# A list-scheduled hybrid decoder step: the scheduler's idea of pauses and landings is changed, half-partition work goes from VectorE to ScalarE and TensorE, and the last scale is kept in PSUM

## The chip, the cores and the metric

One core of a Trainium2 chip runs the whole step in one launch. The metric is the device time of that launch in microseconds (us), over several runs. PE is TensorE, DVE is VectorE, ACT is ScalarE, POOL is GpSimd, SP is the engine that issues most DMAs; PEld is TensorE's weight load.

## The reference

One layer of a decoder for 256 prompt tokens and 8 x 8 sample tokens (320 columns in all), width 2048, all in fp32:

```python
proj = rms_norm(x, ln1_g) @ w_in                     # 2048 -> 7440 columns
o_a = gdn_mixer(...)                                  # 8 gated-DeltaNet heads, chunks of 64 tokens
o_b = rwkv_mixer(...)                                 # 16 RWKV-7 heads, one state of 64 x 64 each
x = x + concatenate([o_a, o_b]) @ w_o
f = (silu(gate) * up) @ w_down                        # gate, up = causal_dwconv(rms_norm(x) @ w_up)
y = rms_norm(x + f, final_g)
```

Both mixers return their recurrent states too. The delta rule needs the solution of a triangular system for each chunk, the RWKV-7 part a state per head, which this kernel updates chunk by chunk: s = decay * (s + k^T u).

## The kernel before

Activations lie transposed, 128 features on partitions and 320 tokens in a row. Each weight piece of 128 x 512 is loaded by SP (`raw`), copied by ACT to a rounded `whi` (line 539) and subtracted by DVE to the rest `wlo` (line 548); PE multiplies `whi` with the high and low part of the activation and `wlo` with the high part (`stream`, lines 554 to 583), so every 128 x 128 tile of weights costs three matmuls of 320 columns. There are 3648 such matmuls up to the end of `w_o` and 6336 in the FFN behind it.

The work before the FFN is the projection, in an order that mixes RWKV pairs of heads (R0 to R7), GDN pairs (G0 to G3) and gates (Z0 to Z3), with the mixers' own small work running between the projection's matmuls. `rwkv` (line 1077) and `gdn` (line 1568) do one pair each: element work on DVE and ACT, a 32 x 32 block solve on DVE (`solve`, line 1374: tiles `xt`, 62 short instructions) with a way through DRAM in front and behind (`scr`, `scx`, `gscr`, `gscx`), a step that joins the blocks on PE (lines 1255 to 1264 and 1678 to 1694), and then four chunks, each of which needs the state that the one before it left (lines 1272 to 1305 and 1702 to 1740).

No engine's order is written by hand. `Prog` (line 167) runs the generators of all parts side by side, keeps a clock for each engine (`clk`), and a time at which every operand is ready (`ready`, line 195: the writer's planned end and a latency from `LAT`, line 104). At each step `run` (line 316) takes of every engine the instruction that can begin first, and appends it to the program. The weight stream has the lowest rank (1000), so it fills PE's planned gaps; its rank is raised when PE would otherwise do too little or has just come back to it (line 337, `vg`). The chip keeps that order on each engine and waits where the plan was too early. Numbers that steer the plan are in `CFG` (line 96). `begin` (line 220) says when an instruction can start: when its engine's clock is past the one before and its operands are ready. `dma` (line 474) plans a landing by bytes, with an additional `lag` where one is given; `dl` is what a DMA adds for its readers.

In the state step of `rwkv` (lines 1285 to 1298) PE forms k^T u in PSUM (`pb`); DVE multiplies the old state by the decay (line 1289) and then adds the decayed product, once for each half of the partitions (line 1298).

At the end, `rms_last` (line 885) gives 1/rms in `rs2`, and 16 tiles are scaled by it: nine by DVE, four by POOL, and the last three by DVE together with the gain (`last`, line 1014). Each goes out by its own DMA, from SP and ACT in turn (lines 1022 to 1024).

Of the kernel before, what the change touches and what calls it, by code (L numbers as in the profile page):

```python
# [19 lines left out]
P = 128  # L20
NTOK = 320
# [74 lines left out]
CFG = dict(es=0, eg=1, ln=1, bl=0, re=(7,), rg=1, gp={3: 5}, nw=(3, 4), b5=4, b4=4, b2=6, c2=9, b1=12, bi=8, raw=7, xt=2, ord='R0 R1 G0 R2 R3 Z0 G1 R4 R5 Z1 G2 R6 R7 Z2 G3 Z3', dl=1900, wr=2, l2=300, ra=3, war=1, vt=150, lw=1, lh=2, s1=9, st=6, m=80, ev=50, sp=0, cv=0, pq=1000, ug=1, sg=0, gv=1023, fs=105, pl=3000, pd=1000, pr=0.4605, ch=100, gs=1.0, hw=3400, ha=0.45, vg=700, pq2=0, fa=1, lk=1)  # L96
# [9 lines left out]


# [59 lines left out]
class Prog:  # L167
    def __init__(self, tc, a, ctx):
# [5 lines left out]
        self.port = {"V": 0.0, "G": 0.0}  # L174
        self.shape, self.work, self.full, self.left_at = (128, 128), [], True, -1e9
# [44 lines left out]
    def begin(self, op):  # L220

        t = max(self.clk[op.key], op.ready)
        return max(t, self.port["G" if op.key == "V" else "V"]) if op.port else t

# [7 lines left out]
    def emit(self, th):  # L232
        op = th.op
        op.fn()
        t = self.begin(op)
        if op.port:
            self.port[op.key] = t + op.cost
# [290 lines left out]
    def wload(self):  # L528
        for p, (ap, w) in enumerate(self.raws):
            t = yield from self.take(self.raw_s, 1)  # L530
            yield self.dma(t[:, :w], ap)
            self.nload = p + 1
            self.raw[p] = t
# [236 lines left out]
    def main(self):  # L770
# [43 lines left out]
        def keys(n, slots):  # L814
            for k in WO[n]:
# [5 lines left out]
                if m is None:  # L821
                    yield self.dma(lo, self.dmx[k])
# [44 lines left out]
        rs2 = fp.tile([P, NTOK], F32, name="rs2")  # L867
        yield self.ms(G, ssa, 0.0)
# [16 lines left out]
        def rms_last(t):  # L885
# [5 lines left out]
            yield from self.rstd(g[:, :NTOK], rs2)  # L891
            self.flags.add("rs2")

# [183 lines left out]
    def rwkv(self, i, box):  # L1077
# [7 lines left out]
        yield self.dma(lw, self.a["lw"][i])  # L1085
# [72 lines left out]
        for h in range(2):  # L1158
            s = slice(64 * h, 64 * h + 64)
            yield self.tt(V, ar[s, :, 0, h], c64(kk)[s], c64(e0)[s], ALU.mult)  # L1160
# [100 lines left out]
        yield self.cp(V, pt_, g[hi, 0:256])  # L1261
# [726 lines left out]
```

## Time and profile before

| what | value |
|---|---|
| three runs | 1780.39, 1783.66 and 1785.14 us, median 1783.66 |
| profiled execution, its own time | 1782.98 us |
| its span (first to last instruction) | 1781.2 us |
| busy share of the span | PE 95%, PEld 92%, DVE 72%, ACT 55%, POOL 10% |
| granted TensorE clock, mean | 0.988 |
| DMA | 256.52 MB, mean 144 GB/s |

The span falls into four stretches by time from its start: the first loads (0 to 36 us), projection and mixers with `w_o` (36 to 834), the FFN (834 to 1766), and the last norm with its stores (1766 to 1781.2). A busy PE says little here, since matmuls overlap each other in the records; what PE waits for and what the other engines do in the second stretch has to be read apart.

### The profile page before, as it was taken

How to read it: one execution, taken by the hardware profiler on the slowest of the kernel's cores; microseconds unless marked ns; L12 is line 12 of the kernel's file. 1: busy time of each engine (PE TensorE's matmuls, PEld its weight loads, DVE VectorE, ACT ScalarE, POOL GpSimd, SP SyncE). 2: the span in 40 equal slices, each digit the busy share in tenths (PEclk: the TensorE clock that was granted, in tenths of full speed). 3: DMA queues.
4: the chain of work that ended last, by engine and by line, in shares of the span. 5: the costliest groups of instructions: out<-in, count | busy, mean ns of one | idle time of the engine just before them, and what ended most of it. 6: DMA issues, size and time to landing. Idle time of an engine off the chain costs nothing.

```text
span 1781.2 us, 33357 instructions
## 1 busy us (share of the span) xinstructions
PE 1700.1 (95%) x11959; PEld 1635.1 (92%) x11959; DVE 1285.2 (72%) x3447; ACT 982.2 (55%) x2281; POOL 180.1 (10%) x482
## 2 busy tenths in 40 slices
PE   8999999899989989999999999999999999999996
PEld 7998889788978888799999999999999999999996
DVE  7989888788978799778766666644466666665444
ACT  7776847575666566546545445433345545455442
POOL 0200000000000000113111111100001111110001
PEclk9999999999999999999999999999999999999998
DMA  6434424344424446355444444455444444445554
GB/s 223 134 126 132 134 95 139 105 134 124 142 82 137 126 125 208 98 187 169 154 148 149 154 147 151 147 152 148 146 155 152 152 146 153 151 147 150 150 144 141
DMA packets 103830, 256.52 MB, mean 144 GB/s; under 512 B 32048, under 2 KB 43056, under 8 KB 103664
## 3 DMA queue, kind: packets, MB, share of 16 engines
q1 hardware_dynamic: 102512, 253.08, 45.5%
q8 instruction: 94, 1.54, 0.4%
q10 hardware_dynamic: 1152, 1.31, 0.2%
q14 instruction: 72, 0.59, 0.1%
HBM read 239.13 MB, written 15.22 MB: 143 GB/s over the span
## 4 chain that ended last, share of the span: by engine, by line
PE 69%; DVE 17%; DMA 7%; ACT 3%; issue 2%; SPq 1%; POOL 0%; DVEq 0%; ACTq 0%; POOLq 0%
PE mm L384 26%; PE rA L384 20%; PE rB L384 19%; DVE wlo L436 4%; PE g L384 3%; DVE b L436 3%; DVE xt L436 2%; DMA b<-scr 2%; ACT b L413 2%; DVE h L436 1%; DMA b<-scx 1%; DVE bi L431 1%; DMA b<-srw 1%; DVE c L431 1%; DVE b L431 1%
## 5 line engine op out<-in xcount | busy, mean ns | idle before, releaser
L413 ACT ACTIVATE whi<-raw 128x512 fp32r<-128x512 f32 (+2 forms) x842 | 520.4, 621 | 592.8 <-PE mm L384 227.8
L436 DVE TENSOR_TENSOR wlo<-raw,whi 128x512 fp32r<-128x512 f32 (+2 forms) x842 | 576.4, 686 | 323.9 <-ACT whi L413 317.3
L384 PE MATMUL mm<-h,whi 128*128 128x320 f32 x2992 | 693.3, 315 | 0.0
L384 PEld LDWEIGHTS mm<-h,whi 128*128 128x128 f32 x2992 | 509.5, 191 | 2.2 <-issue 0.5
L384 PE MATMUL mm<-h,wlo 128*128 128x320 f32 x1496 | 473.4, 316 | 5.0 <-DVE wlo L436 4.9
L384 PEld LDWEIGHTS mm<-h,wlo 128*128 128x128 f32 x1496 | 285.4, 191 | 8.7 <-DVE wlo L436 7.2
L384 PE MATMUL rB<-h,whi 128*128 128x320 f32 x1136 | 250.6, 309 | 0.0
L384 PE MATMUL rA<-h,whi 128*128 128x320 f32 x1136 | 250.6, 309 | 0.0
L384 PEld LDWEIGHTS rB<-h,whi 128*128 128x128 f32 x1136 | 189.8, 188 | 0.1
L384 PEld LDWEIGHTS rA<-h,whi 128*128 128x128 f32 x1136 | 189.8, 188 | 0.0
L384 PE MATMUL rB<-h,wlo 128*128 128x320 f32 x568 | 175.6, 309 | 0.4 <-DVE wlo L436 0.4
L384 PE MATMUL rA<-h,wlo 128*128 128x320 f32 x568 | 175.3, 309 | 0.0
L449 POOL COPY sfo<-f 128x18 f32<-128x18 f32 x88 | 61.3, 697 | 688.6 <-DVE f L436 688.6
L384 PEld LDWEIGHTS rB<-h,wlo 128*128 128x128 f32 x568 | 106.5, 188 | 0.8 <-DVE wlo L436 0.7
L384 PEld LDWEIGHTS rA<-h,wlo 128*128 128x128 f32 x568 | 106.5, 188 | 0.0
L431 DVE SCALAR_TENSOR_TENSOR f<-f,vec,f 128x336 f32<-128x336 f32 x176 | 102.6, 583 | 3.4
L436 DVE TENSOR_TENSOR b<-b,b 80x60 f32<-80x60 f32 (+28 forms) x303 | 80.2, 266 | 9.2 <-ACT b L413 3.7
L384 PE MATMUL rB<-fx,whi 128*128 128x320 f32 x336 | 74.1, 309 | 0.0
L384 PE MATMUL rA<-fx,whi 128*128 128x320 f32 x336 | 74.1, 308 | 0.0
L384 PE MATMUL rA<-b,b 128*32 128x128 f32 (+3 forms) x488 | 56.7, 289 | 15.7 <-DMA b<-srw 5.3
L384 PEld LDWEIGHTS rA<-b,b 128*32 128x32 f32 (+2 forms) x488 | 43.0, 154 | 23.2 <-issue 14.0
L436 DVE TENSOR_TENSOR xt<-xt,b 80x60 f32<-80x60 f32 (+21 forms) x248 | 48.3, 206 | 13.4 <-DMA b<-scr 12.3
(263 smaller groups left out, 2370.2 us busy)
## 6 DMA issues: line engine op xcount, KB each, us to landing
raw<-w_up SPq DMA_DIRECT2D x176, 512.0 KB, 3.7
raw<-w_in SPq DMA_DIRECT2D x116, 512.0 KB, 4.0
raw<-w_dn SPq DMA_DIRECT2D x64, 512.0 KB, 3.5
raw<-w_dn SPq DMA_DIRECT2D x32, 384.0 KB, 3.0
raw<-w_oa SPq DMA_DIRECT2D x16, 512.0 KB, 4.5
b<-sgdn SPq DMA_DIRECT2D x8, 512.0 KB, 5.2
o_sgs<-b SPq DMA_DIRECT2D x8, 512.0 KB, 4.6
raw<-w_ob SPq DMA_DIRECT2D x8, 512.0 KB, 3.8
```

Source lines behind the costliest of these rows:

```text
L384: op = Op("T", cost, (out,), (lhsT, rhs), lambda: self.nc.tensor.matmul(out, lhsT, rhs, start=start, stop=stop))
L413: lambda: self.nc.scalar.activation(out, in_, func, **kw), {AF.Exp: "E", AF.Ln: "L", AF.Silu: "S", AF.Tanh: "T"}.get(func))
L431: lambda: self.V.scalar_tensor_tensor(out, in0, scalar, in1, op0=op0, op1=op1)))
L436: lambda: e.tensor_tensor(out, in0, in1, op=op)))
L449: return self.shared(Op(self.key(e), v if e is self.V else CFG["gs"] * (120 + 3.33 * n), (out,), (in_,), lambda: e.tensor_copy(out, in_)))
```

## The change

- `begin` adds a pause of 114 ns on DVE and 125 ns on ACT where an instruction's operands or result start in another quarter of the partitions than those of the instruction before it (`held`).
- Landings are planned later: 600 ns for the weights (`lr`), 1500 ns for recurrent states, small weights and the mixers' results read back (`ls`), 1500 ns for the GDN solve's way back (`lg`). `vg` goes from 700 to 400. An unused number (`fa`) is gone.
- `mv=127` moves work: the decayed state of `rwkv` is summed by PE in PSUM (an identity matmul with the old state) and copied with the decay as scale by ACT; two products on half the partitions become one DVE product on all and two ACT copies; copies and sign changes in the joining steps and copies of 32 partitions in `triple` go from DVE to ACT. A part for bit 128 is added and not used.
- At the end 1/rms is written to PSUM by ACT for DVE, and a second time to SBUF for POOL. Results go to a tile `yo` of their own; 12 of the 16 tiles are stored in pairs, so ten DMAs take the place of 16.

`CFG` itself differs by `vg=400`, `mv=127, ls=1500, lr=600, lg=1500, hv=114, hs=125`, and `fa=1` left out. The core of the rest:

```diff
@@ -104,6 +104,8 @@
+HELD = {"V": CFG["hv"], "A": CFG["hs"]}
...
@@ -219,8 +222,26 @@
     def begin(self, op):
 
-        t = max(self.clk[op.key], op.ready)
+        t = max(self.clk[op.key] + self.held(op), op.ready)
         return max(t, self.port["G" if op.key == "V" else "V"]) if op.port else t
+
+    def quad(self, ap):
+        return self.psum(ap), self.box(ap)[0] // 32
+
+    def held(self, op):
+
+        if op.key not in HELD or not op.out:
+            return 0
+        r, w = self.reads[op.key], self.writes[op.key]
+        m, q = self.quad(op.out[0])
+        if w.get(m, q) == q and all(r.get(m, q) == q for m, q in map(self.quad, op.ins)):
+            return 0
+        return HELD[op.key]
+
+    def went(self, op):
+        if op.key in HELD and op.out:
+            self.reads[op.key].update(map(self.quad, reversed(op.ins)))
+            self.writes[op.key].update(map(self.quad, op.out))
 
...
     def wload(self):
         for p, (ap, w) in enumerate(self.raws):
             t = yield from self.take(self.raw_s, 1)
-            yield self.dma(t[:, :w], ap)
+            yield self.dma(t[:, :w], ap, lag=CFG["lr"])
...
             yield self.mm(g[:, :NTOK], self.ones, t[:, :NTOK], start=False)
-            yield from self.rstd(g[:, :NTOK], rs2)
+            yield self.act(rs2, g[:, :NTOK], AF.Ln, scale=1.0 / (P * self.KT), bias=self.eps1)
+            yield self.act(g[:, :NTOK], rs2, AF.Exp, scale=-0.5)
+            self.rsp = g[:, :NTOK]
             self.flags.add("rs2")
+            yield self.act(rs2, rs2, AF.Exp, scale=-0.5)
...
         def last(n):
             if n >= NO - 3:
-                yield self.stt(x2[n], x2[n], self.v("lnf", n), rs2, ALU.mult, ALU.mult)
+                yield self.stt(yo[:, n], x2[n], self.v("lnf", n), self.rsp, ALU.mult, ALU.mult)
+            elif n % 3 == 2:
+                yield from self.flag("rs2s")
+                yield self.tt(G, yo[:, n], x2[n], rs2, ALU.mult)
             else:
-                yield self.tt(G if n % 3 == 2 else V, x2[n], x2[n], rs2, ALU.mult)
+                yield self.tt(V, yo[:, n], x2[n], self.rsp, ALU.mult)
             out.append(n)
         for n in range(NO):
             self.spawn(last(n), 3 + n)
-        for n in range(NO):
-            yield lambda: n in out
-            yield self.dma(a["o_y"][:, n], x2[n], self.A if n % 2 else self.S)
+        n = 0
+        while n < NO:
+            w = 2 if 1 < n < NO - 2 else 1
+            yield lambda: all(q in out for q in range(n, n + w))
+            yield self.dma(a["o_y"][:, n:n + w], yo[:, n:n + w], self.A if n // w % 2 else self.S)
...
         for h in range(2):
             s = slice(64 * h, 64 * h + 64)
-            yield self.tt(self.g(2), ar[s, :, 1, h], c64(r)[s], c64(e1)[s], ALU.mult)
+            if CFG["mv"] & 2:
+                if h == 0:
+                    yield self.tt(V, r, r, e1, ALU.mult)
+                yield self.act(ar[s, :, 1, h], c64(r)[s], AF.Copy)
+            else:
+                yield self.tt(self.g(2), ar[s, :, 1, h], c64(r)[s], c64(e1)[s], ALU.mult)
...
-        yield self.cp(V, pt_, g[hi, 0:256])
+        yield self.act(pt_, g[hi, 0:256], AF.Copy) if CFG["mv"] & 8 else self.cp(V, pt_, g[hi, 0:256])
...
             yield self.mm(pb[:, 0:128], xd_[:, 128 * c:128 * c + 128], rr)
             yield from self.corners(vu_[:, 128 * c:128 * c + 128], pb, 0, -1.0)
-            if s0 is not None:
+            if CFG["mv"] & 1:
+                if s0 is not None:
+                    yield self.mm(pb[:, 256:384], ident, two, stop=False)
+            elif s0 is not None:
                 yield self.ts(V, s0[:, 64:128], s0[:, 0:64], dec[:, c:c + 1])
-            yield self.mm(pb[:, 256:384], kt[:, c], vu_[:, 128 * c:128 * c + 128])
+            yield self.mm(pb[:, 256:384], kt[:, c], vu_[:, 128 * c:128 * c + 128], start=not CFG["mv"] & 1 or s0 is None)
             yield self.mm(pa[:, 256:384], at[:, c, 1], vu_[:, 128 * c:128 * c + 128], start=s0 is None)
             new = rr if s0 is None else s0
             for h in range(2):
                 s, x = slice(64 * h, 64 * h + 64), pb[64 * h:64 * h + 64, 256 + 64 * h:320 + 64 * h]
-                if s0 is None:
+                if CFG["mv"] & 1:
+                    yield self.act(new[s, 0:64], x, AF.Copy, scale=dec[s, c:c + 1])
+                elif s0 is None:
                     yield self.ts(V, new[s, 0:64], x, dec[s, c:c + 1])
                 else:
...
-        yield self.dma(ss, self.a["srw"][i])
+        yield self.dma(ss, self.a["srw"][i], lag=CFG["ls"])
...
-            yield self.dma(xc[32 * q:32 * q + 32], sx[q], self.q)
+            yield self.dma(xc[32 * q:32 * q + 32], sx[q], self.q, lag=CFG["lg"])
...
-            yield self.cp(V, xd[s, :, s], xc[s])
+            yield self.act(xd[s, :, s], xc[s], AF.Copy) if CFG["mv"] & 16 else self.cp(V, xd[s, :, s], xc[s])
...
-                    yield self.cp(self.V, o, hi[s].bitcast(F32))
+                    yield self.act(o, hi[s], AF.Copy) if CFG["mv"] & 64 else self.cp(self.V, o, hi[s].bitcast(F32))
```

The scheduler's rules set all orders anew. Two places are shown, in the third chunk of the fourth RWKV pair, and then the end. First DVE before, where `s1_735` is the RWKV state, `rB_775` the PSUM tile with k^T u, `st_503` the decay, `b1_766` the matrix of a GDN pair:

```order
L436 TENSOR_TENSOR b4_736_4327<-b4_736_4327,st_503_2915 128x512
L444 TENSOR_SCALAR s1_735_4326<-s1_735_4326,st_503_2915 128x64
L431 SCALAR_TENSOR_TENSOR b1_766_4508<-g_769_4511,st_685_3927,et_90 128x64 x4
L431 SCALAR_TENSOR_TENSOR s1_735_4326<-rB_775_4530,st_503_2915,s1_735_4326 64x64 x2
L431 SCALAR_TENSOR_TENSOR b1_766_4508<-rB_770_4512,st_685_3927,et_90 128x64
```

The state update stands behind the decay of the old state and four instructions of the GDN pair. In the changed kernel it stands on ACT, where `s1_745` is the state, `rB_768` the PSUM tile, `b2_619` the tile of u:

```order
L435 ACTIVATE b2_619_3560<-rB_768_4543 64x64 x2
L435 ACTIVATE b2_619_3560<-rB_763_4524 64x64
L435 ACTIVATE whi_766_4540<-raw_728_4273 128x512
L435 ACTIVATE s1_745_4355<-rB_768_4543,st_494_2864 64x64 x2
L435 ACTIVATE b1_638_3646,st_639_3647<-rA_760_4508 64x64 x2
L435 ACTIVATE b1_638_3646,st_639_3647<-rA_748_4361 64x64 x2
```

The two halves of the state follow the copies of u with two other ACT instructions between them. PE before, in the same chunk (`mm_739` is the projection):

```order
L384 MATMUL rB_775_4530<-s1_759_4472,b2_645_3694 128x128
L384 MATMUL g_769_4511<-c2_623_3581 64x128
L384 MATMUL g_773_4524<-ones_73,b1_771_4513 64x1 x4
L384 MATMUL mm_739_4348<-h_119_628,whi_732_4291 128x320
L384 MATMUL mm_739_4348<-h_120_629,whi_732_4291 128x320
L384 MATMUL mm_739_4348<-h_119_628,wlo_742_4352 128x320
L384 MATMUL rB_775_4530<-b2_629_3589,b2_628_3588 128x128
L384 MATMUL rA_758_4471<-b2_629_3589,b5_519_3007 128x128
```

Three matmuls of the weight stream stand between the product that gives u and the one that needs it. PE in the changed kernel:

```order
L406 MATMUL rB_768_4543<-s1_761_4509,b2_636_3643 128x128
L406 MATMUL mm_765_4539<-h_83_459,whi_730_4292 128x320
L406 MATMUL mm_765_4539<-h_84_460,whi_730_4292 128x320
L406 MATMUL mm_765_4539<-h_83_459,wlo_742_4335 128x320
L406 MATMUL mm_765_4539<-h_85_467,whi_730_4292 128x320
L406 MATMUL mm_765_4539<-h_86_468,whi_730_4292 128x320
L406 MATMUL g_769_4555<-b4_671_3864,b5_630_3618 32x32 x4
L406 MATMUL rB_768_4543<-s1_745_4355,cst_72 128x128
L406 MATMUL rB_768_4543<-b2_619_3560,b2_618_3559 128x128
L406 MATMUL rA_760_4508<-b2_619_3560,b5_535_3101 128x128
```

Five matmuls of the stream stand there now, the identity matmul (`cst_72`) is new, and parts of a joining step of another pair (`g_769`) stand around it. At the end of the program DVE before has:

```order
L436 TENSOR_TENSOR h_1530_9070<-h_1530_9070,rB_3663_21438 128x320
L436 TENSOR_TENSOR h_1493_8924<-h_1493_8924,rs2_10618 128x320
L436 TENSOR_TENSOR h_1494_8926<-h_1494_8926,rs2_10618 128x320
L436 TENSOR_TENSOR h_1496_8930<-h_1496_8930,rs2_10618 128x320
L436 TENSOR_TENSOR h_1497_8932<-h_1497_8932,rs2_10618 128x320
```

DVE in the changed kernel, where `g_3667` is a PSUM tile:

```order
L458 TENSOR_TENSOR h_1535_9152<-h_1535_9152,rB_3663_21455 128x320
L458 TENSOR_TENSOR yo_10635<-h_1504_9025,g_3667_21474 128x320
L458 TENSOR_TENSOR yo_10635<-h_1511_9036,g_3667_21474 128x320
L458 TENSOR_TENSOR yo_10635<-h_1513_9040,g_3667_21474 128x320
L458 TENSOR_TENSOR yo_10635<-h_1515_9047,g_3667_21474 128x320
```

The order of DVE is the same; the second operand has moved from SBUF to PSUM and the result to `yo`.

## Rows read from the trace of the kernel before

**Rows 1.** Two stretches of the span, from the view of busy time by stretch: us of the stretch, busy us and count of instructions of each engine, granted clock, DMA share, GB/s.

```profile
36.00:834.00 798.00, 739.30 (x5439) 680.58 (x5437) 683.30 (x2321) 509.61 (x1474) 71.97 (x184) 0.98 0.43 133
834.00:1766.00 932.00, 931.57 (x6350) 931.21 (x6350) 568.24 (x1066) 445.83 (x758) 99.57 (x283) 1.00 0.48 149
```

**Rows 2.** The page's part on the chain that ended last: its share of the span by engine.

```profile
PE 69%; DVE 17%; DMA 7%; ACT 3%; issue 2%; SPq 1%; POOL 0%; DVEq 0%; ACTq 0%; POOLq 0%
```

**Rows 3.** What PE waited for between 36 and 834 us: who waited for whom, us in total, times, longest.

```profile
PE g L384 <- DVE b L464: 7.4, 9, 1.5
PE rA L384 <- DMA b<-srw: 5.3, 2, 2.8
PE g L384 <- DVE b L436: 4.9, 7, 1.0
...
PE g L384 <- DVE b L449: 4.5, 5, 1.9
```

**Rows 4.** DVE and then PE in order of time at the third chunk of the fourth RWKV pair (columns as in rows 7).

```profile
339.56 0.85 DVE L431 SCALAR_TENSOR_TENSOR b<-g,st,et 128x64 f32<-128x64 f32 x4
340.33 0.58 DVE L431 SCALAR_TENSOR_TENSOR s<-rB,st,s 64x64 f32<-64x64 f32 x2
...
338.68 0.49 PE L384 MATMUL rB<-b,b 128*128 128x128 f32 x2
...
340.96 0.71 PE L384 MATMUL rA<-s,b 128*128 128x128 f32 x4 [0.72 <-DVE s L431]
```

**Rows 5.** DVE's instructions between 36 and 834 us by form: busy us of the group and mean ns of one, then the idle time before them. `s<-` with `st` is the state step, `b<-bi,b` and `b<-b,b` on 64 partitions are the half products, the rest are copies and sign changes.

```profile
L431 DVE SCALAR_TENSOR_TENSOR s<-rB,st,s 64x64 f32<-64x64 f32 x48 | 13.5, 282 | 2.9 <-PE rB L384 2.3
...
L436 DVE TENSOR_TENSOR b<-b,b 64x320 f32<-64x320 f32 x16 | 7.7, 484 | 0.2
L436 DVE TENSOR_TENSOR b<-bi,b 64x320 f32<-64x320 f32 x16 | 7.7, 483 | 0.3
...
L449 DVE CAST b<-s 32x128 fp32r<-32x128 f32 x32 | 6.9, 216 | 0.7
...
L444 DVE TENSOR_SCALAR s<-s,st 128x64 f32<-128x64 f32 x24 | 5.9, 248 | 0.0
...
L449 DVE COPY c<-b 32x160 f32<-32x160 f32 x16 | 4.8, 301 | 0.2
...
L444 DVE TENSOR_SCALAR s<-rB,st 64x64 f32<-64x64 f32 x16 | 4.5, 283 | 7.7 <-PE rB L384 7.1 <-PE rA L384 0.5
...
L449 DVE COPY b<-g 32x256 f32<-32x256 f32 x8 | 3.4, 430 | 0.2
...
L449 DVE COPY b<-g 32x128 f32<-32x128 f32 x8 | 2.3, 290 | 0.1
```

**Rows 6.** The same view for ACT, the copy of a weight piece, and the forms nearest to those that it gets: from PSUM plain, from PSUM with a scale out of SBUF, and from SBUF.

```profile
L413 ACT ACTIVATE whi<-raw 128x512 fp32r<-128x512 f32 x285 | 176.3, 627 | 129.9 <-PE mm L384 93.9 <-PE g L384 15.6 <-DVE xt L436 6.3
...
L413 ACT ACTIVATE b<-rB 64x64 f32<-64x64 f32 x80 | 17.4, 218 | 11.8 <-PE rB L384 10.3
...
L413 ACT ACTIVATE c<-g,st 64x128 f32<-64x128 f32 x40 | 14.5, 363 | 6.4 <-DVE st L436 3.0 <-PE g L396 2.8
...
L413 ACT ACTIVATE b<-s 32x128 fp32r<-32x128 f32 x32 | 9.8, 307 | 0.5
...
L413 ACT ACTIVATE b<-rA 64x128 f32<-64x128 f32 x16 | 4.4, 273 | 9.0 <-PE rA L384 8.7
...
L413 ACT ACTIVATE b<-g 64x256 f32<-64x256 f32 x8 | 3.1, 382 | 0.2
...
L413 ACT ACTIVATE b<-b 64x320 f32<-64x320 f32 x1 | 0.5, 457 | 0.0
```

**Rows 7.** DVE's and then ACT's instructions in order of time: start us, us, engine, line, operation, tiles, form, count, and in brackets the idle time before it. The transpose and the ACT instruction at 105.89 work on other partitions than their neighbours.

```profile
318.14 0.43 DVE L464 STREAM_TRANSPOSE b<-b 32x256 f32<-32x256 f32 x1 [0.39 <-DMA b<-scx]
318.61 0.22 DVE L436 TENSOR_TENSOR xt<-xt 80x65 f32<-80x65 f32 x1
318.75 0.15 DVE L431 SCALAR_TENSOR_TENSOR st<-st 128x5 f32<-128x5 f32 x1
...
105.39 0.47 ACT L413 ACTIVATE b<-b 128x320 f32<-128x320 f32 x1
105.89 0.38 ACT L413 ACTIVATE b<-g 64x256 f32<-64x256 f32 x1
106.17 0.21 ACT L413 ACTIVATE bi<-stc 128x24 f32<-128x24 f32 x1
```

**Rows 8.** PE's matmuls of 128 x 128 x 128 between 36 and 834 us by form, the group's busy time first.

```profile
L384 PE MATMUL g<-b,b 128*128 128x128 f32 x160 | 23.0, 275 | 0.0
L384 PE MATMUL rB<-b,b 128*128 128x128 f32 x64 | 14.7, 313 | 1.1 <-ACT b L413 1.0
```

**Rows 9.** The end of the program in order of time.

```profile
1766.38 0.49 DVE L436 TENSOR_TENSOR h<-h,rB 128x320 f32<-128x320 f32 x1 [5.13 <-PE rB L384]
...
1768.89 0.47 ACT L413 ACTIVATE rs<-rs 128x320 f32<-128x320 f32 x1
1769.39 6.36 DVE L436 TENSOR_TENSOR h<-h,rs 128x320 f32<-128x320 f32 x9 [2.52 <-ACT rs L413]
1769.43 4.35 POOL L436 TENSOR_TENSOR h<-h,rs 128x320 f32<-128x320 f32 x4 [11.19 <-ACT rs L413]
...
1775.67 1.47 DVE L431 SCALAR_TENSOR_TENSOR h<-h,vec,rs 128x320 f32<-128x320 f32 x3
```

More of the change, by code (lines that the diff above doesn't have):

```diff
@@ L174, in __init__ @@
         self.port = {"V": 0.0, "G": 0.0}
+        self.reads, self.writes = {k: {} for k in HELD}, {k: {} for k in HELD}
         self.shape, self.work, self.full, self.left_at = (128, 128), [], True, -1e9
@@ L235, in emit @@
         t = self.begin(op)
+        self.went(op)
         if op.port:
@@ L821, in keys @@
                 if m is None:
-                    yield self.dma(lo, self.dmx[k])
+                    yield self.dma(lo, self.dmx[k], lag=CFG["ls"])
                 self.spawn(key(k, m, hi, lo), 3)
@@ L867, in main @@
         rs2 = fp.tile([P, NTOK], F32, name="rs2")
+        yo = fp.tile([P, NO, NTOK], F32, name="yo")
         yield self.ms(G, ssa, 0.0)
@@ L890, in rms_last @@
             yield self.mm(g[:, :NTOK], self.ones, t[:, :NTOK], start=False)
-            yield from self.rstd(g[:, :NTOK], rs2)
+            yield self.act(rs2, g[:, :NTOK], AF.Ln, scale=1.0 / (P * self.KT), bias=self.eps1)
+            yield self.act(g[:, :NTOK], rs2, AF.Exp, scale=-0.5)
+            self.rsp = g[:, :NTOK]
             self.flags.add("rs2")
+            yield self.act(rs2, rs2, AF.Exp, scale=-0.5)
+            self.flags.add("rs2s")
         def sq_last(n, t):
@@ L1021, in main @@
             self.spawn(last(n), 3 + n)
-        for n in range(NO):
-            yield lambda: n in out
-            yield self.dma(a["o_y"][:, n], x2[n], self.A if n % 2 else self.S)
+        n = 0
[3 more added lines that the diff above has]
+            yield self.dma(a["o_y"][:, n:n + w], yo[:, n:n + w], self.A if n // w % 2 else self.S)
+            n += w
     def setup_mixers(self, ml):
@@ L1084, in rwkv @@
         lw, lh = self.lw.take(), self.lh.take()
-        yield self.dma(lw, self.a["lw"][i])
+        yield self.dma(lw, self.a["lw"][i], lag=CFG["ls"])
         yield self.act(lh[:, 0:384], lw, AF.Copy)
@@ L1159, in rwkv @@
             s = slice(64 * h, 64 * h + 64)
-            yield self.tt(V, ar[s, :, 0, h], c64(kk)[s], c64(e0)[s], ALU.mult)
+            if CFG["mv"] & 4:
+                if h == 0:
+                    yield self.tt(V, kk, kk, e0, ALU.mult)
+                yield self.act(ar[s, :, 0, h], c64(kk)[s], AF.Copy)
+            else:
+                yield self.tt(V, ar[s, :, 0, h], c64(kk)[s], c64(e0)[s], ALU.mult)
         for d, x in ((dec[:, 0:4], c64(e1[:, :NPR])[:, :, 63]), (dec[:, 4:12], b8(e1)[:, :, 7])):
@@ L1260, in rwkv @@
         pt_ = mt_[hi, 256:512]
-        yield self.cp(V, pt_, g[hi, 0:256])
+        yield self.act(pt_, g[hi, 0:256], AF.Copy) if CFG["mv"] & 8 else self.cp(V, pt_, g[hi, 0:256])
         for m in range(8):
             yield self.mm(g[lo, 256 + 32 * m:288 + 32 * m], pt_[:, 32 * m:32 * m + 32], xd[hi, m, 32:64])
-        yield self.ts(V, xd[lo, 0:8, 32:64], g[lo, 256:512].rearrange("p (m x) -> p m x", x=32), -1.0)
+        gx = g[lo, 256:512].rearrange("p (m x) -> p m x", x=32)
+        yield self.act(xd[lo, 0:8, 32:64], gx, AF.Copy, scale=-1.0) if CFG["mv"] & 8 else self.ts(V, xd[lo, 0:8, 32:64], gx, -1.0)
         gps.give()
@@ L1651, in gdn @@
         yield self.dma(mt_[0:80, :], scr.unsqueeze(0).to_broadcast([GG, NS, 1024]), self.q, lag=CFG["pl"])
+        if CFG["mv"] & 128:
+            yield from self.want(b1)
+            qc_ = b1.take()
+            qc = qc_[:, 0:320].rearrange("p (c x) -> p c x", c=5)
         for c in range(5):
             o = 128 * (c % 4)
+            if CFG["mv"] & 128:
+                yield self.stt(qc[:, c], gg[c // 4][:, o + 64:o + 128], s_[:, c:c + 1], self.et[:, p, c], ALU.mult, ALU.mult)
+                continue
             for h in range(2):
@@ L1658, in gdn @@
         self.rB.give()
+        if CFG["mv"] & 128:
+            for h in range(2):
+                s = slice(64 * h, 64 * h + 64)
+                yield self.act(qkd[s, :, s], qc[s], AF.Copy)
+            b1.give(qc_)
         hd["sq"] = 0
@@ L1686, in gdn @@
             hi = slice(64 * h + 32, 64 * h + 64)
-            yield self.cp(V, pt_[hi], g[hi, 0:128])
+            yield self.act(pt_[hi], g[hi, 0:128], AF.Copy) if CFG["mv"] & 32 else self.cp(V, pt_[hi], g[hi, 0:128])
         for h in range(2):
@@ L1693, in gdn @@
             lo, hi = slice(64 * h, 64 * h + 32), slice(64 * h + 32, 64 * h + 64)
-            yield self.ts(V, xd[lo, 0:4, hi], g[lo, 128:256].rearrange("p (c t) -> p c t", c=4), -1.0)
+            gx = g[lo, 128:256].rearrange("p (c t) -> p c t", c=4)
+            yield self.act(xd[lo, 0:4, hi], gx, AF.Copy, scale=-1.0) if CFG["mv"] & 32 else self.ts(V, xd[lo, 0:4, hi], gx, -1.0)
         gps.give()
@@ L1812, in gdn_sample @@
         for h in range(2):
-            yield self.dma(sv[h], self.a["sgdn"][2 * p + h])
+            yield self.dma(sv[h], self.a["sgdn"][2 * p + h], lag=CFG["ls"])
         yield from self.want(b4)
```

2 lines of the change are left out of this document (1 added, 1 removed).

## The prediction

> **What bounds the kernel now.** I read the busy time by stretch first. From 834 to 1766 us PE is busy for 931.57 of 932 us at a granted clock of 1.00, 6350 matmuls in a row [rows 1]: nothing that the change moves between VectorE and ScalarE can shorten this stretch. From 36 to 834 us PE is busy for 739.30 of 798 us, so 59 us are open idle time, the clock is 0.98, and DVE is busy for 683.30 us against ACT's 509.61 [rows 1]. DVE is 86% busy in a stretch in which PE often needs its results, so DVE has little room to catch up. The chain of waits says the same: DVE holds 17% of the span, ACT 3%, DMA 7%, PE 69% [rows 2]. In us, DVE's part is 0.17 x 1781 = 303. The end of the program has 8 of these (0.49 + 6.36 + 1.47) [rows 9] and I take 5 for the first loads, which leaves 290 between 36 and 834 us. PE's part is 1229 us; the FFN alone is 932 of them, so only some 297 us of the 798 before it are PE's on the chain. The second stretch is thus bound by a chain that goes to and fro between PE and DVE. The waits of PE agree: the longest groups end with DVE (7.4, 4.9 and 4.5 us), and one with the load of an RWKV state, two waits of 5.3 us in all [rows 3].
>
> One place shows how it happens. PE issues the two parts of the product k^T u at 338.68 us. DVE, in the planned order, first does four instructions of a GDN pair (339.56, 0.85 us) and begins the state update at 340.33. PE's next product with that state begins at 340.96, after 0.72 us of idle time [rows 4].
>
> **What the plan did not know.** Neighbours on the same partitions overlap: the short instruction at 318.75 begins 0.08 us before the end of the one at 318.61 + 0.22. Behind the transpose on other partitions (318.14 + 0.43 = 318.57) the next begins 0.04 us late. A change of partitions thus costs DVE about 0.12 us. On ACT the same reading gives 0.03 us late (105.39 + 0.47 to 105.89) and 0.10 us early (106.27 to 106.17), a pause of 0.13 us [rows 7]. I counted such changes in the two orders by the rule that the diff adds: up to the FFN, DVE goes from 378 to 141 and ACT from 482 to 679. The plan of before missed 378 x 0.12 = 45 us on DVE, and every wait that it laid out behind them came too early.
>
> The Trainium skill's page VectorE: DVE Perf Modes says in its section The DRAIN you can't avoid that after each VectorE instruction the next waits until the pipe is empty, unless it is one that is not held. By the first half alone the number of changes would not matter. The overlap of 0.08 us speaks for the second half [rows 7].
>
> **The change, part by part.**
>
> DVE loses 184 instructions. The state step loses 48 of 282 ns, 24 of 248 and 16 of 283: 23.9 us. The 32 half products of 484 ns become 16 of the same 320 columns: 7.7 us. The joining steps lose 16 of 256 columns at about 430 ns, 16 of 128 columns at about 290 (I price the sign changes as the copies), and 16 copies of 301: 16.3 us. The 32 casts of 216 ns are 6.9 us. That is 55 us of records [rows 5]. Each record overlaps its neighbour by 0.08 us, so 184 x 0.08 = 15 us of it were never the engine's own: 40 us. With 237 pauses fewer at 0.12 (28 us), DVE gets 68 us back.
>
> ACT gains 176 there. 64 state copies from PSUM: 218 ns plain [rows 6]; a scale out of SBUF makes 363 of 273 at 64 x 128, so 90 ns more [rows 6]: 64 x 308 = 19.7 us. 32 copies of 64 x 320 at 457 ns: 14.6. 16 copies of 256 columns at 382, 16 of 128 at 273, 16 of 160 at about 310, 32 of 128 at 307: 25.2 [rows 6]. Together 59.5 us, less 176 x 0.10 overlap, plus 197 pauses at 0.13: 67.5 us. So the work is moved, not saved: 68 us from an engine with 115 us of idle time in that stretch to one with 288 [rows 1].
>
> PE gains 24 identity matmuls (three chunks in each of eight pairs), two records each. Nothing in the trace is an identity matmul behind another product; the nearest are 128 x 128 x 128 groups: 23.0 us for 160 records (0.144) and 14.7 for 64 (0.23) [rows 8]. That is 7 to 11 us; I take 7, since the new ones stand directly ahead of a product of the same form, as those of the first group do.
>
> On the chain: DVE's 290 us shrink by 68/683 = 10%, so by 29. ACT's 53 us (3%) grow by 67.5/510 = 13%, so by 7. PE's 297 us of 739 are 40%, so 3 of the 7 us count. Its bounds from the same rows: all 68 us of DVE if DVE were the chain throughout, and none if PE's own order were; the share by the chain lies between, and nearer to none.
>
> Later landings: issues keep their places among the loads, only readers are planned later, and PE's order gets other work ahead of them. The two state waits of 5.3 us [rows 3] should go but for one: 4 us gained. Weights planned 600 ns later and 1500 ns later for the GDN way back can only make their readers wait in the plan, behind work that is ready; I put them at nothing, with 5 us either way, about one wait group of rows 3. `vg` likewise.
>
> The end: nine DVE products take 6.36 us beside four POOL products of 4.35 us, 0.71 us each where the sum with a PSUM operand takes 0.49 [rows 9]; three more follow in 1.47. So 12 products take 7.75 us, from 1769.39 to 1777.14; at 0.49 each they would take 5.9, and I take 6.5, nearer to that end, since the second operand comes from PSUM as in the sum. POOL begins one ACT instruction of 0.47 us later and ends at about 1774.3, ahead of DVE. Gain 1.2 us; bounds 2 gained and 1 lost, if the paired stores wait for the later of their two tiles.
>
> The Trainium skill's page SBUF — State Buffer (section on practical consequences) has a VectorE instruction with two SBUF inputs contend with a GpSimd instruction that reads SBUF, and one with a single SBUF input not. By that rule the 0.71 falls to 0.49 and about 2 us go; without it, if 0.71 had another cause, nothing goes. The two rates in rows 9 agree with it.
>
> Sum: -29 + 7 + 3 - 4 - 1.2 = -24. The profiled execution took 1782.98 us, its span 1781.2; the median of the runs shown is 1783.66, 0.7 above. So 1759 us for the execution, and 1759 to 1760 for the median: I say 1759.
>
> **The rivals.**
>
> A, the forecast: 1745 to 1772, chance 0.60.
>
> B, DVE is nearly the whole limit of the second stretch. For it: 86% busy, and PE's longest waits end with it. Against it: 297 us of the chain are PE's, 125 DMA's. All 68 us would go, PE's 7 come on top: 1783 - 68 + 7 - 4 - 1 = 1717; with two thirds of it 1740. Chance 0.18.
>
> C, the order is bound elsewhere: by the ways through DRAM (7% of the chain, 125 us, untouched) and by PE's own small products, and the DVE time that is gone was beside them. This is also the case in which the plan's new numbers fit no better than the old. Then +7 of PE, -4, -1: 1785. Chance 0.10.
>
> D, slower: ACT becomes what PE waits for. In the changed order a weight copy `whi` and one copy more stand between u and the state's halves; at 0.627 us for a `whi` [rows 6] each of 32 chunks could lose 0.6 us, 20 us in all, and PE's 7 come on top, against DVE gains off the chain: 1783 + 20 + 7 - 13 = 1797 with half the forecast's DVE and landing gains kept. It decides once the halves begin on average more than 1.1 us behind the product, as DVE's did in rows 4. Against it: ACT idles 288 us there. Chance 0.09.
>
> The rest (0.03) is spread. About 0.3% or 5.4 us is what a measurement of this kernel can tell from no change. Faster by more: A, B and some of the rest, 0.80. Within it: C and edges, 0.10. Slower: D and edges, 0.10. The range for 8 in 10 reaches from B's milder part to C: 1732 to 1784.
>
> **What would show it.** Right: DVE's busy time before the FFN down by 40 us or more and ACT's up by about as much, the FFN beginning some 20 us earlier, PE's waits for `b`, `st` and `s` of DVE shorter in sum, no wait for `b<-srw` over 1 us, and products at the end of 0.5 us. Wrong: the FFN begins where it did while DVE idles (C), or PE's and `wlo`'s waits for ACT grow by 15 us or more (D). The forecast falls if the FFN's own 932 us change by more than 2.

## The result and the profile after

The changed kernel takes 1727.53 us (median of four runs, 1725.06 to 1734.07), the kernel before 1782.03 in the same comparison (1778.06 to 1785.14). The ratio is 0.9701, with a 95% interval from 0.9667 to 0.9735. The gain is 54 us; the forecast was 24, and its range ended at 1732.

The profiled execution of the changed kernel took 1728.42 us with a span of 1726.6. First the busy time by stretch (columns as in [rows 1]), the FFN's stretch being cut where it now begins:

```profile
36.00:781.50 745.50, 725.83 (x5476) 677.61 (x5474) 619.76 (x2131) 567.54 (x1642) 71.62 (x186) 0.98 0.46 142
781.50:1714.50 933.00, 932.16 (x6352) 931.31 (x6351) 568.95 (x1067) 446.29 (x759) 96.42 (x283) 1.00 0.47 149
```

The FFN is what it was: PE is busy for 932.16 of 933 us. The stretch ahead of it went from 798 us [rows 1] to 745.5. PE's open idle time there fell from 59 us to 20. That is 39 of the 52.5 us; the other 13.5 are PE's busy time (725.83 after 739.30 us), although it has the identity matmuls on top. Busy time can hide waits: in the FFN 66 matmuls with records of 0.31 us start within 9.67 us, one every 0.147 us, so a matmul that starts up to 0.16 us late leaves no idle time in the profile. How much of the 13.5 us this is was not taken apart. DVE is busy for 619.76 us where it was for 683.30, ACT for 567.54 where it was for 509.61. So the work did move as the forecast said (63.5 us less on DVE, 58 more on ACT; the forecast counted 55 and 59.5 us of records), and the FFN begins some 52 us earlier, not 20. One instruction near its start can be found in both kernels. In the kernel before:

```profile
834.47 0.41 PE L384 MATMUL rB<-h,wlo 128*128 128x320 f32 x1 [0.43 <-DVE wlo L436]
```

In the changed kernel:

```profile
781.95 0.41 PE L406 MATMUL rB<-h,wlo 128*128 128x320 f32 x1 [0.16 <-DVE wlo L458]
```

That is 52.5 us of the 54.6 by which the span is shorter. The rest is at the end of the program, here in the changed kernel (columns as in [rows 9]):

```profile
1716.36 0.44 ACT L435 ACTIVATE g<-rs 128x320 f32<-128x320 f32 x1
1716.84 0.47 ACT L435 ACTIVATE rs<-rs 128x320 f32<-128x320 f32 x1
1716.84 3.67 DVE L458 TENSOR_TENSOR yo<-h,g 128x320 f32<-128x320 f32 x9 [2.49 <-ACT g L435]
...
1717.38 3.34 POOL L458 TENSOR_TENSOR yo<-h,rs 128x320 f32<-128x320 f32 x4 [11.66 <-ACT rs L435]
...
1720.42 1.46 DVE L453 SCALAR_TENSOR_TENSOR yo<-h,vec,g 128x320 f32<-128x320 f32 x3
```

DVE's 12 products end 5.04 us after they begin, where they took 7.75 [rows 9]. In the kernel before, the nine products were of two kinds: four that began while POOL was at work on its own took 1.14 to 1.15 us each, the other five 0.48 to 0.49. In the changed kernel all nine take 0.48 to 0.49, also those beside POOL. The chain that ended last, by engine, as in [rows 2]:

```profile
PE 72%; ACT 9%; DVE 8%; DMA 4%; issue 1%; SPq 0%; DVEq 0%; POOL 0%; ACTq 0%
```

DVE's share fell from 17% to 8%, which is 303 to 138 us, and ACT's rose from 3% to 9%. The experiments show that such a share is no price. What PE waited for between 36 and 780 us, the longest groups (columns as in [rows 3]):

```profile
PE g L406 <- DVE b L486: 6.0, 6, 2.1
PE rB L406 <- ACT b L435: 4.2, 4, 3.8
PE rB L406 <- ACT s L435: 2.2, 5, 0.5
PE g L406 <- DVE b L458: 1.9, 5, 0.9
```

Of the groups of [rows 3] the transposes (L464, now L486) are nearly as they were, 6.0 us after 7.4; the wait for `b<-srw` and DVE's copies are gone.

### The profile page after: what moved, and what is told of

Read it like the earlier page. It is cut to its first block, busy times and chain, and to the rows that moved or that the text cites. A ratio compares the mean times of both kernels' runs of the same rounds, so it can differ in the third digit from the quotient of the medians.

```text
span 1726.6 us, 33397 instructions
## 1 busy us (share of the span) xinstructions
PE 1688.6 (98%) x12007; PEld 1633.1 (95%) x12007; DVE 1222.0 (71%) x3263; ACT 1043.7 (60%) x2458; POOL 174.6 (10%) x482
## 4 chain that ended last, share of the span: by engine, by line
PE 72%; ACT 9%; DVE 8%; DMA 4%; issue 1%; SPq 0%; DVEq 0%; POOL 0%; ACTq 0%
PE mm L406 28%; PE rA L406 20%; PE rB L406 20%; ACT b L435 4%; PE g L406 4%; DVE wlo L458 2%; DMA b<-scr 2%; DVE xt L458 2%; ACT s L435 2%; ACT whi L435 1%; DVE b L458 1%; ACT L435 1%; DVE bi L453 1%; DMA scx<-xt 1%; ACT bi L435 1%
## 5 line engine op out<-in xcount | busy, mean ns | idle before, releaser
L458 DVE TENSOR_TENSOR b<-b,b 80x66 f32<-80x66 f32 (+27 forms) x295 | 75.8, 259 | 11.2 <-ACT b L435 6.1
L479 POOL MEMSET b<- 128x4 f32 (+6 forms) x52 | 27.2, 534 | 359.6 <-PE rB L406 148.9
L435 ACT ACTIVATE f<-f,vec 128x336 f32<-128x336 f32 x88 | 50.8, 577 | 9.3 <-DVE f L458 0.6
```

Of the source, the lines that this page charges most:

```text
L435: lambda: self.nc.scalar.activation(out, in_, func, **kw), {AF.Exp: "E", AF.Ln: "L", AF.Silu: "S", AF.Tanh: "T"}.get(func))
L458: lambda: e.tensor_tensor(out, in0, in1, op=op)))
L479: return Op(self.key(e), 36 + 0.83 * self.width(out), (out,), (), lambda: e.memset(out, v))
```

## The experiments

The theory at the start was that of the work: DVE gets rid of pieces on which PE waits. The rival was that of the plan: the scheduler knows the engines' pauses and lays its orders out right. A third had the later landings carry the gain. Each kernel is the changed one with other numbers in `CFG`, except one. `mv=0` puts all moved work back, `hv` and `hs` are DVE's and ACT's pauses, `ls`, `lr` and `lg` the landings. All keep the new end.

All results first. W is the work (old, or moved). Waits are sums over the groups of the view of PE's waits between 36 and 780 us, by what ended them (those ended by POOL, by PE itself, or by nothing that the profile shows are left out). The kernel before had medians from 1781.0 to 1784.5 us in the comparisons behind this table, so 3 us between two kernels of different comparisons say nothing. "Lost" is (1 - mean granted clock) x span, the median over a kernel's runs, in us.

| kernel | W | pauses | landings | us | by DVE | by ACT | by DMA | lost |
|---|---|---|---|---|---|---|---|---|
| before | old | none | old | 1782.0 | 37.7 | 10.4 | 5.3 | 27 |
| e3_end_only | old | none | old | 1779.6 | 35.6 | 9.0 | 5.0 | 27 |
| e13_old_act | old | ACT | old | 1782.3 | 32.8 | 5.3 | 4.5 | 43 |
| e16_old_dve | old | DVE | old | 1767.9 | 28.4 | 13.9 | 0.5 | 28 |
| e9_old_pauses | old | both | old | 1750.9 | 22.8 | 9.7 | 1.4 | 30 |
| e10_old_landings | old | none | new | 1768.3 | 32.4 | 8.2 | 0.7 | 24 |
| e1_old_work | old | both | new | 1738.9 | 16.6 | 12.2 | 2.7 | 22 |
| e8_state_only | state step | both | new | 1748.3 | 14.8 | 12.1 | 3.9 | 25 |
| e2_old_plan | moved | none | old | 1775.3 | 17.0 | 17.2 | 3.5 | 20 |
| e4_no_pauses | moved | none | new | 1774.0 | 13.8 | 23.1 | 0.4 | 18 |
| e11_dve_pauses | moved | DVE | new | 1763.3 | 12.4 | 22.4 | 1.8 | 11 |
| e12_act_pauses | moved | ACT | new | 1732.0 | 13.1 | 3.4 | 0.2 | 15 |
| e5_no_landings | moved | both | old | 1739.9 | 14.5 | 7.0 | 3.3 | 14 |
| after | moved | both | new | 1727.5 | 11.4 | 7.5 | 0.2 | 17 |
| e7_no_state | all but the state step | both | new | 1722.6 | 10.3 | 10.3 | 0.6 | 9 |

### The change taken apart: work, plan, end

The first three kernels undo one part each.

```diff
-mv=127, vg=400, ls=1500, lr=600, lg=1500, hv=114, hs=125
+mv=0, vg=400, ls=1500, lr=600, lg=1500, hv=114, hs=125      e1_old_work
+mv=127, vg=700, ls=0, lr=0, lg=0, hv=0, hs=0                e2_old_plan
+mv=0, vg=700, ls=0, lr=0, lg=0, hv=0, hs=0                  e3_end_only
```

> The new scheduler numbers and the new end, but all work on the engines of before (mv=0). Theory P (the plan: the gain comes from pauses and landings being planned): at most 1745 us, the FFN begins 35 us or more earlier than before. Theory M (the moves: the gain comes from the 68 us taken off DVE): 1770 us or more, the FFN begins no more than 10 us earlier. If both are needed: between.

> The moves of work and the new end, but the scheduler numbers of before (no pauses, no added landings, vg=700). P: 1765 us or more. M: at most 1745 us. If both are needed: between.

> The kernel before with the new end alone; every order up to the last scale is that of before. Both theories: 1.5 to 2.5 us less than before, read from the stretch behind the last projection product (14.2 us from ACT's square to the end in before, 12.2 in the changed kernel).

Measured: 1738.93 with the new plan and the old work (ratio 0.977, 0.9753 to 0.9786), 1775.29 with the moved work and the old plan (0.9965, 0.9946 to 0.9985), 1779.58 with the end alone (0.9984, 0.9967 to 1.0002). Under the new plan the old work gains 41 us, and the FFN begins some 42 us earlier than before; under the old plan the moves gain 4 us (e3 to e2). The moves did relieve DVE. Its busy time falls from 643 to 601 us of the 744, and here is the chain of e2_old_plan:

```profile
PE 69%; DVE 12%; ACT 10%; DMA 4%; issue 3%; POOL 1%; SPq 0%; DVEq 0%; ACTq 0%; POOLq 0%
```

DVE's 17% became 12%, ACT's 3% became 10% [rows 2], and in the table PE's waits for DVE halve while those for ACT double: of 19 us less for DVE 8 come back for ACT. PE's idle time up to the FFN falls by 12 us from e3 to e2 (56 to 44), but its busy time rises by 6 (737 to 743), with 11.8 us of records for the identity matmuls that are new. The relief is thus spent in part on the other engine and in part on PE itself.

### Pauses or landings

```diff
-ls=1500, lr=600, lg=1500, hv=114, hs=125
+ls=0, lr=0, lg=0, hv=114, hs=125             e5_no_landings
+ls=1500, lr=600, lg=1500, hv=0, hs=0         e4_no_pauses
+mv=0, vg=700, ls=0, lr=0, lg=0               e9_old_pauses
+mv=0, vg=700, hv=0, hs=0                     e10_old_landings
```

> The changed kernel without the later landings (ls, lr and lg at 0). P with the pauses as its cause: within 8 us of the changed kernel, 1720 to 1736. P with the landings as its cause: 1745 us or more. M: within 8 us of the changed kernel too.

> The changed kernel without the planned pauses (hv and hs at 0), with the moves, the later landings and vg=400. Theory P1 (the pauses are the larger part of the plan's gain): 1755 us or more. P2 (the landings are): within 10 us of the changed kernel, at most 1738.

> The work and landings of before and vg=700, with the pauses alone and the new end. P1: 1738 to 1755 us, most of the 41 us that the new plan gave to the old work (1739 against 1780 with the new end alone). P2: 1765 us or more.

> The work of before and vg=700, without pauses, with the later landings alone and the new end. P1: 1765 us or more. P2: 1738 to 1755 us.

Measured: without landings 1739.89 (0.9777, 0.9758 to 0.9795), without pauses 1774.03 (0.9955, 0.9938 to 0.9973), and with the old work the pauses alone 1750.92 (0.9828, 0.9795 to 0.9862), the landings alone 1768.26 (0.9931, 0.9912 to 0.9951). Without landings the time lies between the two ranges of its expectation, so neither held there; the other three came out for the pauses. The pauses are worth 29 us with the old work (1779.6 to 1750.9) and 46.5 with the moved work and the later landings (1774.0 to 1727.5). The landings are worth 11 us with the old work (1779.6 to 1768.3) and 12 with the moved work and pauses (1739.9 to 1727.5), but with the moved work and no pauses 1 us (1775.3 to 1774.0, `vg` changed too).

The table also shows what the moves are worth under each plan. With planned pauses it is 11 us, with the old landings (1750.9 to 1739.9) and with the new ones (1738.9 to 1727.5; in the first pair `vg` changes too). Without pauses it is 4 us gained with the old landings (1779.6 to 1775.3) and 6 lost with the new (1768.3 to 1774.0, `vg` changed too). A clear gain of the moves is seen only where the plan knows the pauses. They take changes of partitions from DVE and give ACT more of them (482 to 679). Adding one part at a time, in one of the possible orders, gives 1779.6, pauses 1750.9, landings and `vg` 1738.9, moves 1727.5. (`vg` was not tried alone.) Here are PE's waits in e4_no_pauses:

```profile
PE rA L406 <- ACT b L435: 6.5, 12, 1.3
PE g L406 <- ACT b L435: 6.0, 10, 1.2
...
PE g L406 <- DVE b L486: 3.5, 3, 1.4
```

The two longest groups now end with ACT, in many short waits of 0.5 to 0.6 us.

### Which engine's pauses

```diff
-hv=114, hs=125
+hv=114, hs=0                                          e11_dve_pauses
+hv=0, hs=125                                          e12_act_pauses
+mv=0, vg=700, ls=0, lr=0, lg=0, hv=0, hs=125          e13_old_act
+mv=0, vg=700, ls=0, lr=0, lg=0, hv=114, hs=0          e16_old_dve
```

> The changed kernel with pauses planned on DVE alone (hs=0). In the changed order DVE has 141 changes of partitions (16 us) and ACT 679 (85 us). If the gain follows the pause that is missing in the plan: close to the kernel without pauses, 1760 to 1774 us. If DVE's planned clock is what counts, as the engine with the least room: 1730 to 1745 us.

> The changed kernel with pauses planned on ACT alone (hv=0). If the gain follows the missing pause: 1728 to 1740 us. If DVE's planned clock is what counts: 1755 us or more.

> The work, landings and vg of before and the new end, with pauses planned on ACT alone (hv=0). Its order of before has 482 changes on ACT (63 us) and 378 on DVE (45 us). If ACT's planned clock is what counts for the old work too: 1748 to 1758 us, near the kernel with both pauses (1751). If the two share the gain by their sums: 1760 to 1768 us. If DVE's pauses carry it there: 1770 us or more.

> The old work and old landings, with DVE's pauses alone in the plan (ACT's 0), and the new end. With both pauses this was 1751, with ACT's alone 1782, without any 1780. Theory 1 (of the two engines the one that is late in the old order decides, and that is DVE): 1749 to 1757, nearly all of the gain with DVE's pauses alone. Theory 2 (only both together give the plan the right relation between the engines, as in the changed order): 1765 to 1780.

With the moved work DVE's pauses alone leave 1763.26 (0.9898, 0.9876 to 0.992), ACT's alone give nearly everything, 1732.01 (0.9734, 0.9699 to 0.9769). Both expectations that follow the missing pause held. That fits the counts of the prediction: 679 changes of partitions on ACT are 85 us that the plan would miss, 141 on DVE only 16. PE's waits in e12_act_pauses, the longest and ACT's longest:

```profile
PE g L406 <- DVE xt L458: 4.1, 3, 1.5
...
PE g L406 <- ACT et L435: 1.5, 1, 1.5
PE rB L406 <- ACT s L435: 1.5, 3, 0.5
```

The groups of 6.5 and 6.0 us are gone; the sum of what ACT ends falls from 23.1 to 3.4 us, and e11, again without ACT's pauses, has 22.4.

With the old work ACT's pauses alone give nothing (1782.33; 0.9989, 0.9976 to 1.0002), DVE's 12 us (1767.94; 0.9917, 0.9897 to 0.9938), both 29. Neither theory of e16 holds in full: the first asked for 1749 to 1757, and 1767.9 is inside the second's range but shows a real gain. Each engine's pauses reduce the waits which that engine ends (ACT 9.0 to 5.3, DVE 35.6 to 28.4), and both together do more than the sum of the two. So the size of the gain can't be read from the missed us alone: with the old work ACT misses more (63 us against 45). That e13 gains nothing although its waits shrink by some 7 us has a visible companion: its clock, below.

### The right amount, and the right place

If the plan needs only slower engines on the whole, the same pauses spread evenly must do. And if planning late is good in itself, more must do better.

```diff
-        if op.key not in HELD or not op.out:
+        if op.key not in HELD or not op.out or "ffn" in self.flags:
             return 0
-        r, w = self.reads[op.key], self.writes[op.key]
-        m, q = self.quad(op.out[0])
-        if w.get(m, q) == q and all(r.get(m, q) == q for m, q in map(self.quad, op.ins)):
-            return 0
-        return HELD[op.key]
+        return {"V": 7.3, "A": 56.7}[op.key]                  u1_mean_pause
...
+        self.flags.add("ffn")
```

```diff
-hv=114, hs=125
+hv=171, hs=188                                                e14_more_pause
```

> The changed kernel with the same planned pause in sum up to the FFN, but spread evenly: 7.3 ns on each DVE instruction and 56.7 ns on each ACT one instead of 114 and 125 at the changes of partitions. If what counts is that the engines' planned clocks are right on the whole: within 8 us of the changed kernel, 1720 to 1736. If each pause has to stand at its place: 1740 us or more.

> The changed kernel with pauses planned half as long again (171 and 188 ns instead of 114 and 125). If what helps is that the plan is right: 1730 us or more, none faster than the changed kernel beyond its spread. If any slower plan helps: at most 1722 us.

The even pause gives 1745.66 (0.9806, 0.9773 to 0.984): 28 of the 46.5 us. So, as far as one such order can show, more than half of the gain is that the planned clocks of DVE and ACT no longer run ahead of the chip, and the other 18 us come from putting each pause where it falls. With pauses of one and a half times the size the kernel takes 1738.42 (0.9742, 0.972 to 0.9764): 11 us slower than with the right ones. That planning still later doesn't help is shown; that it costs 11 us is not, since another order alone can cost 9 (below).

### The state step, and more moves

```diff
-mv=127
+mv=126      e7_no_state
+mv=1        e8_state_only
+mv=254      e17_mv254
```

> The changed kernel with the RWKV state step left on DVE (mv=126), so without the identity matmuls. If the state step carries the gain of the moves under the new plan (11 us between 1739 and 1728): 1735 us or more. If the copies and half products carry it: 1724 to 1732 us.

> The changed kernel with the state step as its only move (everything else as in the old work, all plan numbers new). The old work under the new plan was 1739. Theory 1 (the state step through PE and ACT is a loss of its own, as its removal from the changed kernel, 5 us faster, says): 1741 to 1748. Theory 2 (it costs only because ACT is loaded by the other moves): 1733 to 1739.

> The changed kernel without the state step and with the part for bit 128, which moves a half-partition product of the GDN pairs in the same manner. Theory 1 (moves that leave the chunk's chain alone give a little each): 1715 to 1722. Theory 2 (ACT is full enough by now): 1723 to 1732.

Without the state step's move the kernel takes 1722.6 (0.966, 0.9642 to 0.9677): 5 us faster than the changed kernel, the fastest of all, and below both ranges of its expectation, each of which had the state step worth something or nothing, not a loss. The state step as the only move takes 1748.31 (0.9797, 0.9769 to 0.9826), 9 us slower than no move at all (e1). So the move that took most from DVE (23.9 us of records) gained nothing. Its instructions cost what was forecast, ACT's 64 copies first, then the identity matmuls, in the changed kernel between 36 and 781.5 us (columns as in [rows 5]):

```profile
L435 ACT ACTIVATE s<-rB,st 64x64 f32<-64x64 f32 x64 | 19.8, 309 | 15.1 <-PE rB L406 14.3
...
L406 PE MATMUL rB<-s,cst 128*128 128x128 f32 x48 | 10.3, 298 | 3.8 <-ACT b L435 3.8
```

309 ns against 308 forecast, and 10.3 us of PE against 7 to 11. New is what stands behind the bar. ACT sits idle for 14.3 us ahead of the copies, until PE's product is there, and PE for 3.8 us ahead of the identity matmul; DVE in e7 waits 2.6 us for the same step. Adding the part for bit 128 instead gives 1726.43 (0.9686, 0.9667 to 0.9705), which is not better than e7.

### How far an order's luck reaches

Every change of a number sets all orders anew, so two kernels were run that change an unrelated one, `m`, from 80 to 85, in the changed kernel and in e3.

```diff
-m=80
+m=85        n6_m85; with mv=0 and the old plan: n5_old_m85
```

> A control: the changed kernel with the small margin on PE's operands at 85 ns instead of 80, which sets another order by the same rules. Plan right on the whole: 1720 to 1740 us, the spread of such orders. A lucky order in the changed kernel: 1745 us or more.

> The same control for the kernel before with the new end: margin 85 instead of 80. Plan wrong on the whole: 1768 us or more. An unlucky order in the kernel before: 1760 us or less.

1730.32 (0.9716, 0.9695 to 0.9737) and 1788.29 (1.0045, 1.0023 to 1.0067): 3 us above the changed kernel and 9 above e3. The gap between the changed kernel and the old work under the old plan stands (58 us here, 52 between after and e3), and so do the pauses' 29 and 46.5 us, but differences of some 5 us between two single orders, the moves' 4 in the old plan or the state step's 5, are no more than such a draw can make. The 11 and 12 us of the moves and of the landings lie not far above it; each was found in more than one pair of orders. For the state step two kernels with different orders, e7 and e8, point the same way; I take it for no gain, and a loss as likely.

## Why the prediction was wrong, step by step

**What bounds the kernel.** Right: the stretch before the FFN held it, the FFN did not change. The reading of it was wrong. DVE's 17% of the chain were taken as DVE being the limit. In e4 the share is 8%, as after the change, and the time is 1774:

```profile
PE 71%; DVE 8%; ACT 7%; DMA 5%; issue 2%; POOL 0%; SPq 0%; DVEq 0%; ACTq 0%; POOLq 0%
```

The chain named the engine that PE waited for in that order; taking work from it did not give the time back.

**The step that failed.** It is the one between "What the plan did not know" and the sum. The prediction wrote that the plan of before missed 45 us of pauses on DVE "and every wait that it laid out behind them came too early", and then gave that no term. The pauses appear only as 28 us of DVE's own time, part of the 68 that it gets back. Yet the pauses were there on the chip before and after; what changed is that the order allows for them. This missing term measured 29 us with the old work and 46.5 with the moved work, the largest of all. The lines for it were already quoted: 45 us on DVE and 482 x 0.13 = 63 on ACT by which the plan's clocks ran ahead, in a stretch in which PE stood idle for 59. These counts don't give its size (e13 and e16), but they gave no reason to put it at nothing.

**VectorE -29, ScalarE +7, TensorE +3.** The work's sizes were right within ten us (DVE's busy time fell by 63.5 against 55 us of records); their credit was not. Net -19 was expected; measured are -4 with the old plan and -11 with the new pauses and landings, to which the state step added nothing. With the old plan 8 us of DVE's relief came back as waits for ACT (9.0 to 17.2 us) and 6 as PE's own busy time. The first is rival D's mechanism at work. It did not turn the sign there. From e10 to e4 the moves do lose 6 us, which is no more than an order's luck can make. With ACT's pauses in the plan it is gone (3.4 in e12): D took ACT's lateness as given and left out that a plan which knows it can place other work on PE ahead of ACT's copies. (D's sum is off by itself: half of the forecast's 29 + 4 is 16.5, not 13, so 1793 instead of 1797.)

**Landings -4.** Mis-sized: -11 and -12, and -1 with the moved work and no pauses. The two waits for the states went as forecast (5.0 us ended by DMA in e3, 0.7 in e10). The weights and the way back, priced at nothing with 5 us either way, may hold the rest; they were not tried one by one, so this stays open.

**The end -1.2.** Mis-sized a little: from ACT's square to the end of the span it takes 12.2 us after 14.2, so -2. The 0.71 us was a mean of two rates. Beside POOL's four products DVE began one every 1.06 us, and one every 0.40 us once POOL was done, with both inputs still in SBUF. The 0.49 taken as the floor is the length of one record; neighbours overlap by 0.08 us, as the prediction had read elsewhere, so 0.40 from start to start was the rate to use. Now all nine keep it, beside POOL too, and POOL's went from 1.09 to 0.83. The Trainium skill's page SBUF — State Buffer (practical consequences) says that a VectorE instruction with at most one SBUF input, outside the 2-port modes, doesn't contend with GpSimd. The trace agrees: both engines got faster. Of the 2.7 us by which DVE's products are shorter 0.7 are lost behind them: from the last product to the end of the span it takes 4.7 us after 4.1.

**The rivals.** B's time (1717 to 1740) holds the result by luck, through a mechanism that the runs refute: DVE's relief gives 11 us at most, not 45 to 68. C had two halves. That the DVE time taken away was mostly beside the limit is near to what e2 shows (4 us); that the plan's new numbers fit no better than the old is refuted by e9 alone. The measured sum is -2 for the end, -29 for the pauses, -12 for landings and `vg`, -11 for the moves, together -54. In another order of adding them the terms differ: the moves first give -4 and the whole plan then -48.

**The signs.** Nearly all that was named as a sign of being right came: DVE's busy time fell by more than 40 us, PE's waits for DVE went from 37.7 to 11.4 us, those for `b<-srw` are gone, the FFN kept its length. They could not tell the theories apart. In e1, which moves no work, PE's waits for DVE fall to 16.6 us as well.

## What to carry to other kernels

Where a planner sets the orders, compare its durations with the trace first, pauses between instructions included: an engine whose plan runs ahead makes its readers wait, also where it has room (ACT, in e4). A share of the chain or of the waits names who was late and is no price; moving that engine's work without mending the plan moved part of the wait to the next engine here. Give a change of the plan a term of its own. The idle time of the engine that waits (59 us here) tells what is at stake, and part of the gain came on top, out of its busy time. And name signs that only one of the theories would leave.

## What was not expected of the hardware

TensorE's granted clock moves with these orders, and its share was no term of the prediction. In the changed kernel, between 142 and 160 us (columns as in [rows 1]):

```profile
142.00:144.00 2.00, 1.92 (x14) 1.65 (x12) 2.00 (x6) 1.62 (x5) 0.00 (x0) 1.00 0.40 70
144.00:146.00 2.00, 1.35 (x23) 1.15 (x23) 1.94 (x9) 0.61 (x2) 0.00 (x0) 1.00 0.70 244
146.00:148.00 2.00, 2.00 (x30) 1.50 (x29) 1.88 (x7) 0.89 (x4) 0.00 (x0) 0.88 0.23 49
148.00:150.00 2.00, 2.00 (x13) 1.62 (x9) 1.25 (x8) 0.16 (x1) 0.00 (x0) 0.50 0.93 306
...
156.00:158.00 2.00, 2.00 (x13) 2.00 (x12) 1.86 (x9) 0.43 (x2) 0.00 (x0) 0.56 0.35 51
158.00:160.00 2.00, 2.00 (x18) 2.00 (x17) 1.71 (x7) 0.98 (x4) 0.00 (x0) 1.00 0.25 94
```

PE idles for 0.65 us of the two from 144 us. In the stretch from 146 us the clock begins to fall, from 148 us it is 0.50, the lower of its two levels (1.2 GHz), and from 158 us it is back at 1.00; PE has no idle time in any of these stretches. How often this happens differs from kernel to kernel. The windows from 36 to 780 us of e7_no_state and then of e13_old_act show the two ends:

```profile
36.00:780.00 744.00, 722.06 (x5477) 672.29 (x5477) 644.93 (x2231) 549.31 (x1590) 75.56 (x191) 1.00 0.47 144
```

```profile
36.00:780.00 744.00, 698.74 (x5076) 639.80 (x5075) 633.16 (x2246) 479.22 (x1419) 58.59 (x170) 0.95 0.42 129
```

It differs between executions of one kernel too. Of the 62 runs of the kernel before in the experiments' comparisons, the quickest (1773.6 us) had a mean clock of 0.990 and the slowest (1789.26) 0.981, and a line through them rises by 0.59 us for each us lost as the table counts it. By that slope, an estimate, e7's 8.7 us less of lost clock are 5 us, as much as it gained on the changed kernel, and e13's 16 us more than e3's are 9.5, which would have hidden a gain of about 7 by ACT's pauses. The gain of the pauses together is not the clock's: the lost us go from 27 to 30 with the old work (e3 to e9) and from 18 to 17 with the moved work (e4 to after). No run held the clock still, so whether the state step's move loses by its waits or by the clock that follows from them stays open; that it gains nothing is measured.

ACT was found to pause at a change of partitions as DVE does, 0.13 us against 0.12 [rows 7], and e11 and e12 show that with the moved work its pauses are the ones that matter; with the old work it takes both (e9, e13, e16).
